# Attention's loop in a gated encoder step: lows, transposes and values at other steps, one reciprocal for two heads, shared score tiles, LayerNorm's own temporaries

## The chip, the cores and the metric

The kernel runs on one core of one Trainium2 chip. Its time is the device time of one execution in microseconds (us); lower is better. Of several executions the median is given. One further execution is recorded by the profiler; it has its own time.

## The reference

One step of an encoder layer with two branches on one RMS-normed input `h` (1024 prompt tokens, 32 sample tokens with 512 cached keys, model width 1024, 16 heads of 64):

```python
q = rmsnorm(h @ w_q, q_g) / 8 ; k = rmsnorm(h @ w_k, k_g) ; v = h @ w_v       # per head
logf = log_sigmoid(h @ w_f + b_f) ; c = cumsum(logf)
s = q @ k.T + c[t] - c[s]            # causal mask
o = softmax(s) @ v
u = (h @ w_ua) * sigmoid(h @ w_ub)
conv = causal_dwconv(u, w_dw, width 31) + b_dw
ya = (o * silu(h @ w_ga)) @ w_pa
yb = (silu(layernorm(conv, ln_g, ln_b)) * silu(h @ w_gb)) @ w_pb
y = x + (sigmoid(h @ w_ma) * ya + sigmoid(h @ w_mb) * yb) @ w_out
```

Everything is float32 outside; inside, each product is made of three matmuls of high and low halves (hi x hi, lo x hi, hi x lo).

## The kernel before

Activations lie with channels on the 128 partitions and the 1056 tokens along the free dimension, in three chunks of 352 columns (`CH`). The kernel runs in stages: input split and the projections u, v, k, q and the first gates (0 to 581 us); **attention, interleaved with the rest of the gate projections** (581 to 1021 us); output projections (from 1021 us). The change lies in the second stage alone.

*Units.* A unit is one block of 128 queries of one head: `units` runs over the 8 pairs of heads, within a pair over the blocks in the order `MORD = (3, 1, 2, 0)` (two query blocks each, so i = 6, 7, 2, 3, 4, 5, 0, 1), and within a block over the two heads (e = 0, 1). A unit has w = 128 (i + 1) keys. That gives 128 units, 16 for a pair of heads; here "narrow" means i up to 3, w up to 512. At loop step k these stand, in this order:

- `scores` of unit k (L1220 to L1222): matmuls into a PSUM tile psS, 1024 fp32 columns wide, of which there are two;
- `high` of unit k-2 (L1243, ScalarE): the probabilities times a factor, as f16, into the tile PH (four buffers);
- half of the step's fill: pieces of gate projections (L188), three matmuls each, whose number goes with the width of the unit;
- `top` of k (L1226, VectorE, the row maximum) and `soft` of k (L1231, ScalarE, the exponential into P, four buffers, with the row sum);
- `low` of k-2: the rest after the high part, on VectorE for the first head (L1252), on GpSimd in two instructions for the second (L1249, L1250);
- `factor` of k-1 (L1236, L1237, VectorE): one reciprocal of the row sum and one scaling;
- the step's events: loads of the next heads, and for each block of four units `values` (L1280, matmuls with the transposed probabilities PT) at `LAG` = 6 steps after the first unit's step + 3, and `gated` a step later;
- the other half of the fill, then `turn` of k-2 (L1260): a transposing DMA from PH to PT, issued by SyncE.

Each engine takes its instructions in the order in which they are written here; SyncE's queue, too, which also issues the weight loads, the next heads' loads and the stores of gate tiles.

*Beats.* Each piece of fill is a beat. A beat runs what is due: the preparation of the next weights (`stage`: squares and their sum; `total`: a small matmul; `power`; `split` and `rest`: L141, L146), and taps. A tap (L379, VectorE) is one of 31 terms of the depthwise convolution for one channel block f; `pace["rate"]` (`R_A` = 0.15 in this stage) says how many run in a beat. After the last tap of f the result y is stored (`kept`), and `sums(f)` subtracts the shift from y in place (L345) and adds y to the running mean (L352) and, later, its square (L359). After channel block 7 these give LayerNorm's statistics: `layernorm` runs one piece in each loop step and takes its temporaries from the tiles `t` (`t352`, three buffers), which also hold the gate projections' results until they are stored.

Of the kernel before, what the change touches and what calls it, by code (L numbers as in the profile page):

```python
# [34 lines left out]
R_U, R_V, R_QK, R_G, R_A = 0.21, 0.18, 0.165, 0.23, 0.15  # L35
NWARM = 34
PS14 = 2.0 ** 14
LAG = 6
# [19 lines left out]
def build(tc, xT, xt, wv, wf, ckT, cv, clT, stT, vec, cst, yT, kT, vO, lfO, cpT, csT):  # L58
# [33 lines left out]
    class Batch:  # L92
# [21 lines left out]
        def stage(self, i):  # L114
# [6 lines left out]
            if i == 1:  # L121
                nc.gpsimd.tensor_copy(self.topb, self.tops)
# [103 lines left out]
    def begin():  # L226
# [10 lines left out]
        elif b.n == 2:  # L237
# [5 lines left out]
            if lag > 1:  # L243
                jobs[:2] = [(23, b.total), (23, b.power)]
# [124 lines left out]
    def conv_taps(f):  # L369
        u = us.pop(f)  # L370

        def tap(i):
# [9 lines left out]
            if i == KC - 1:  # L382
                kept(f, y)

# [3 lines left out]
        if f == 7:  # L388
            taps.extend(pend + items)
# [788 lines left out]
    taps.extend(sums(7))  # L1178
# [26 lines left out]
    class Unit:  # L1205
# [6 lines left out]
        def scores(self):  # L1212
# [3 lines left out]
            self.ps = ps = psS.tile([128, T], F32, name="psS", tag="S")  # L1216
# [7 lines left out]
        def top(self):  # L1224
            self.nm = ap.tile([128, 3], F32, name="nm", tag="nm", bufs=6)
            nc.vector.tensor_reduce(self.nm[:, 0:1], self.ps[:, :self.w], axis=AX.X, op=ALU.max, negate=True)  # L1226

        def soft(self):
            self.P = ap.tile([128, T], F32, name="P", tag="P", bufs=4)
            with tc.issue_after(sides["tables"].ins):  # L1230
                nc.scalar.activation(self.P[:, :self.w], self.ps[:, :self.w], AF.Exp, bias=self.nm[:, 0:1],  # L1231
                                     accum_out=self.nm[:, 1:2])

        def factor(self):
            nm = self.nm
            nc.vector.reciprocal(nm[:, 2:3], nm[:, 1:2])  # L1236
            nc.vector.tensor_scalar(nm[:, 2:3], nm[:, 2:3], PS14, None, op0=ALU.mult)  # L1237

        def high(self):
            n = self.i + 1  # L1240
            self.H = ap.tile([128, 8, 2, 128], F16, name="PH", tag="PH", bufs=4)
            self.P3 = self.P[:, :self.w].rearrange("p (j k) -> p j k", j=n)
            nc.scalar.mul(self.H[:, :n, 0, :], self.P3, self.nm[:, 2:3])  # L1243

        def low(self):
            n = self.i + 1
            f = self.nm[:, 2:3]
# [50 lines left out]
    def layernorm():  # L1298

        shift = sides["shift"]  # L1300
# [4 lines left out]
        for c in range(3):  # L1305
            sl = csl(c)
            t = t352("t", 3)
# [3 lines left out]
            nc.tensor.matmul(pm[:, :CH], ones_f, rstd[:, sl], start=True, stop=True)  # L1311
            nc.vector.scalar_tensor_tensor(rstd[:, sl], pm[:, :CH], 1.0 / D, t, op0=ALU.mult, op1=ALU.subtract)
            nc.vector.tensor_add(mean[:, sl], mean[:, sl], shift[:, sl])
            nc.vector.tensor_scalar(rstd[:, sl], rstd[:, sl], EPS, None, op0=ALU.add)
        for c in range(6):
            sl = slice(c * CH // 2, c * CH // 2 + CH // 2)
            v, y = rstd[:, sl], t352("t", 3)[:, :CH // 2]
# [3 lines left out]
            w = t352("t", 3)[:, :CH // 2]  # L1321
# [19 lines left out]
    rate = (24 * NFILL - 30) / sum(u.w + WB for u in units)  # L1341
# [453 lines left out]
```

## Time and profile before

| | |
|---|---|
| median of three executions | 1311.63 us (1310.82 to 1311.67) |
| profiled execution | 1317.82 us, span of its instructions 1314.7 us |
| TensorE (PE) busy | 1249.7 us, 95% |
| VectorE (DVE) busy | 1013.1 us, 77% |
| ScalarE (ACT) busy | 732.9 us, 56% |
| GpSimd (POOL) busy | 632.4 us, 48% |
| DMA | 213.66 MB, mean 163 GB/s |

The rows of the trace in this document are read so. A group of instructions: line of the kernel, engine, operation, tiles (out<-in), shapes, count | busy us, mean ns of one | the engine's idle time just before them, and what ended it. A wait: who waited <- for whom: us in total, times, longest. A stretch of busy time: start:end, length, then for PE, PEld (weight loads), DVE, ACT and POOL busy us (count), the granted TensorE clock, the DMA engines' busy share, GB/s. A line of the timeline: start us, length us, engine, line, operation, tiles, count, and in brackets the idle time before it.

### The profile page before, as it was taken

The page shows a single profiled execution, that of the slowest core. Times are in us where ns is not written, and L with a number is a line of the kernel's source. Part 1 is how long each engine was busy: PE and PEld are TensorE (multiplying, and loading weights), DVE is VectorE, ACT ScalarE, POOL GpSimd, SP SyncE. Part 2 cuts the span into 40 slices and gives each one's busy share as a digit, 9 for nine tenths or more (in the row PEclk, how much of TensorE's full clock was granted, in tenths as well). Part 3 has the DMA queues.
Part 4 walks back from the last instruction along what each step waited for, and adds up shares of the span by engine and source line. Part 5 has one row for each costly group of instructions (what it writes and reads, how often), then busy time and mean ns, then how long its engine had stood idle before and what let it go on. Part 6 is the DMA issues. An engine that isn't in the chain of part 4 may idle for free.

```text
span 1314.7 us, 25051 instructions
## 1 busy us (share of the span) xinstructions
PE 1249.7 (95%) x9270; PEld 929.2 (71%) x9270; DVE 1013.1 (77%) x1526; ACT 732.9 (56%) x1353; POOL 632.4 (48%) x590
## 2 busy tenths in 40 slices
PE   8999999999999999998888898979799999999998
PEld 5677776666666666665555565646466799999998
DVE  6799899888988998889778798857566496156664
ACT  6555555867686865556556555656565665133320
POOL 4057574728474741015545355443444277165562
PEclk9999999999999999999989999989899999999999
DMA  7344242425343464629988898978987987444462
GB/s 258 100 131 118 79 129 62 122 66 142 95 118 109 116 196 156 195 82 192 201 200 188 197 227 203 211 181 191 205 189 158 345 263 242 146 132 156 119 213 70
DMA packets 275161, 213.66 MB, mean 163 GB/s; under 512 B 188512, under 2 KB 241632, under 8 KB 275040
## 3 DMA queue, kind: packets, MB, share of 16 engines
q1 hardware_dynamic: 274896, 212.01, 60.9%
q8 instruction: 72, 1.18, 0.4%
q14 instruction: 49, 0.40, 0.1%
q10 hardware_dynamic: 144, 0.07, 0.0%
HBM read 115.04 MB, written 59.22 MB: 133 GB/s over the span
## 4 chain that ended last, share of the span: by engine, by line
PE 71%; DVE 8%; issue 6%; DMA 6%; POOL 5%; ACT 3%; SPq 0%; POOLq 0%; ACTq 0%; DVEq 0%
PE pj L188 52%; PE pjv L813 7%; PE pj L1625 6%; DMA PT<-PH 4%; PE po L1280 2%; POOL PH L1250 2%; POOL P L1249 2%; DVE PH L1252 2%; DVE nm L1226 1%; DVE wl L146 1%; DVE y L379 1%; DMA s_y<-y 1%; POOL wh L141 1%; PE psS L1220 1%; PE psS L1221 1%
## 5 line engine op out<-in xcount | busy, mean ns | idle before, releaser
L188 PE MATMUL pj<-xh,wh 128*128 128x352 f16 (+2 forms) x1536 | 485.0, 316 | 0.6 <-DVE qn L959 0.5
L188 PE MATMUL pj<-xl,wh 128*128 128x352 f16 (+2 forms) x1536 | 484.0, 315 | 1.4 <-DVE xl L599 1.3
L188 PE MATMUL pj<-xh,wl 128*128 128x352 f16 (+2 forms) x1536 | 484.3, 315 | 0.1
L188 PEld LDWEIGHTS <-wh 128*128 128x128 f16 x3072 | 302.5, 98 | 166.1 <-issue 3.6
L379 DVE SCALAR_TENSOR_TENSOR y<-u,vec_t,y 128x1086 f32<-128x1086 f32 x240 | 360.2, 1502 | 3.9 <-ACT y L376 0.9
L188 PEld LDWEIGHTS <-wl 128*128 128x128 f16 x1536 | 151.3, 98 | 69.1 <-issue 1.0
L146 DVE SCALAR_TENSOR_TENSOR wl<-raw,sc,wh 128x384 f16<-128x384 f32 x188 | 142.7, 780 | 26.7 <-ACT wh L143 25.3
L1231 ACT ACTIVATE P<-psS,nm 128x1024 f32<-128x1024 f32 (+7 forms) x128 | 94.0, 734 | 111.7 <-DVE nm L1236 53.9
L1249 POOL TENSOR_SCALAR P<-P,nm 128x896 f32<-128x896 f32 (+3 forms) x64 | 65.8, 1028 | 181.7 <-ACT PH L1243 177.2
L1243 ACT ACTIVATE PH<-P,nm 128x1024 f16<-128x1024 f32 (+7 forms) x128 | 98.5, 770 | 46.7 <-DMA PT<-PH 24.5
L1226 DVE TENSOR_REDUCE nm<-psS 128x1 f32<-128x1024 f32 (+7 forms) x128 | 96.1, 751 | 30.7 <-PE psS L1222 30.5
L180 POOL TENSOR_TENSOR wl<-raw,wh 128x384 fp32r<-128x384 f32 (+1 forms) x51 | 64.4, 1287 | 72.8 <-ACT wh L177 50.9
L1220 PE MATMUL psS<-KB,QB 128*128 128x512 f16 (+2 forms) x192 | 63.7, 332 | 35.7 <-ACT P L1231 35.4
L1250 POOL TENSOR_TENSOR PH<-P,PH 128x896 f16<-128x896 f32 (+3 forms) x64 | 89.5, 1398 | 4.9
L944 POOL TENSOR_TENSOR sql<-sqf,sqh 128x352 fp32r<-128x352 f32 x48 | 54.0, 1127 | 66.0 <-ACT sqh L941 65.8
L1252 DVE SCALAR_TENSOR_TENSOR PH<-P,nm,PH 128x896 f16<-128x896 f32 (+3 forms) x64 | 61.2, 956 | 28.6 <-ACT PH L1243 28.6
L1280 PE MATMUL po<-PT,Vh 128*64 128x256 f16 (+1 forms) x640 | 63.6, 285 | 15.0 <-DMA PT<-PH 15.0
L813 PE MATMUL pjv<-vwh,xh 128*128 128x260 f16 x256 | 70.1, 274 | 0.0
L813 PE MATMUL pjv<-vwl,xh 128*128 128x260 f16 x256 | 70.0, 273 | 0.0
L813 PE MATMUL pjv<-vwh,xl 128*128 128x260 f16 x256 | 69.9, 273 | 0.0
L970 POOL TENSOR_TENSOR ql<-qn,qh 128x352 f16<-128x352 f32 (+1 forms) x48 | 63.8, 1344 | 8.8 <-ACT qh L969 8.6
L119 ACT ACTIVATE junk<-raw 128x1024 bf16<-128x1024 f32 x62 | 65.0, 1049 | 0.1
(299 smaller groups left out, 2628.7 us busy)
## 6 DMA issues: line engine op xcount, KB each, us to landing
raw<-wf SPq DMA_DIRECT2D x92, 512.0 KB
kT<-kun SPq DMA_DIRECT2D x8, 528.0 KB
s_ga<-t SPq DMA_DIRECT2D x24, 176.0 KB
s_gb<-t SPq DMA_DIRECT2D x24, 176.0 KB
s_ma<-t SPq DMA_DIRECT2D x24, 176.0 KB
s_mb<-t SPq DMA_DIRECT2D x24, 176.0 KB
sma<-s_ma SPq DMA_DIRECT2D x24, 176.0 KB
y<-s_y SPq DMA_DIRECT2D x8, 528.0 KB
```

The source lines that it names most:

```text
L146: nc.vector.scalar_tensor_tensor(wl[:, ks, :], raw[:, ks, :], self.s[:, i:i + 1], wh[:, ks, :], op0=ALU.mult, op1=ALU.subtract)
L188: nc.tensor.matmul(ps, a[:, kt, :], b(kt, sl), start=(first and n == 0), stop=(last and n == N - 1))
L379: t = nc.vector.scalar_tensor_tensor(y, u[:, i:i + CW], w, y, op0=ALU.mult, op1=ALU.add)
L813: nc.tensor.matmul(ps[:, :VC], a, b, start=(n == 0), stop=(n == 23))
L1226: nc.vector.tensor_reduce(self.nm[:, 0:1], self.ps[:, :self.w], axis=AX.X, op=ALU.max, negate=True)
L1231: nc.scalar.activation(self.P[:, :self.w], self.ps[:, :self.w], AF.Exp, bias=self.nm[:, 0:1], accum_out=self.nm[:, 1:2])
L1243: nc.scalar.mul(self.H[:, :n, 0, :], self.P3, self.nm[:, 2:3])
L1249: nc.gpsimd.tensor_scalar(self.P3, self.P3, f, 1.0, op0=ALU.mult, op1=ALU.mult)
L1250: nc.gpsimd.tensor_sub(self.H[:, :n, 1, :], self.P3, self.H[:, :n, 0, :])
L1252: nc.vector.scalar_tensor_tensor(self.H[:, :n, 1, :], self.P3, f, self.H[:, :n, 0, :], op0=ALU.mult, op1=ALU.subtract)
L1280: nc.tensor.matmul(po[64 * e:64 * e + 64, 128 * ii.start:256], v[:, j, 64 * e:64 * e + 64], pt[:, ii, e, j, x, :], start=(j == 0 and n == ...
L1625: nc.tensor.matmul(pss[c][:, :HC], a[:, k, :], x, start=(not more and kt == 0 and n == 0), stop=(kt == 3 and n == 2), skip_group_check=more)
```

## The change

- `soft`, `top`: the small tile `nm` is one for both heads of a pair (maxima in columns 0 and 1, sums in 2 and 3, factors in 4 and 5). `factor` runs once for two heads, at the even steps.
- `scores`: for narrow units both heads of a pair share one psS tile, the first head in columns 0 to 511, the second in 512 to 1023.
- `high` is of unit k-3 instead of k-2, PH has five buffers (`PHB`); `low` is of k-3 and stands at the step's end; `turn` is called for two units at a time, k-5 and k-4, at even steps; the values come two steps later (`LAG` = 8); the loop has four more steps.
- The gate fill in the loop: 36 pieces instead of 30 are left for its end.
- Taps: rate 0.18 instead of 0.15; for f = 7 the sums of block 6 come after eight taps instead of three; the sums of block 7 come 28 beats after its last tap instead of at once.
- Weights in this stage: the sum of squares is cast on ScalarE instead of GpSimd, and its `total` comes at beat 19 instead of 23.
- `layernorm` has temporaries of its own (`lt`, three buffers of 176 columns), and its second sum is made in six pieces instead of three.

```diff
-R_U, R_V, R_QK, R_G, R_A = 0.21, 0.18, 0.165, 0.23, 0.15
+R_U, R_V, R_QK, R_G, R_A = 0.21, 0.18, 0.165, 0.23, 0.18
-LAG = 6
+LAG = 8
+PHB = 5
...
-                nc.gpsimd.tensor_copy(self.topb, self.tops)
+                if sides.get("cast") == "pool":
+                    nc.scalar.copy(self.topb, self.tops)
+                else:
+                    nc.gpsimd.tensor_copy(self.topb, self.tops)
...
-                jobs[:2] = [(23, b.total), (23, b.power)]
+                jobs[:2] = [(19, b.total), (23, b.power)]
...
             if i == KC - 1:
                 kept(f, y)
+                if f == 7:
+                    later(28, lambda: [fn() for fn in sums(7)])
...
         if f == 7:
-            taps.extend(pend + items)
+            taps.extend(items[:8] + pend + items[8:])
...
-    taps.extend(sums(7))
...
-            self.ps = ps = psS.tile([128, T], F32, name="psS", tag="S")
+            if i > 3:
+                self.ps = ps = psS.tile([128, T], F32, name="psS", tag="S")
+            else:
+                if not self.e:
+                    self.pair.ps = psS.tile([128, T], F32, name="psS", tag="S")
+                self.ps = ps = self.pair.ps[:, 512 * self.e:512 * self.e + 512]
...
         def top(self):
-            self.nm = ap.tile([128, 3], F32, name="nm", tag="nm", bufs=6)
-            nc.vector.tensor_reduce(self.nm[:, 0:1], self.ps[:, :self.w], axis=AX.X, op=ALU.max, negate=True)
+            e = self.e
+            if not e:
+                self.pair.nm = ap.tile([128, 6], F32, name="nm", tag="nm", bufs=4)
+            self.nm = self.pair.nm
+            nc.vector.tensor_reduce(self.nm[:, e:e + 1], self.ps[:, :self.w], axis=AX.X, op=ALU.max, negate=True)
...
-            nc.vector.reciprocal(nm[:, 2:3], nm[:, 1:2])
-            nc.vector.tensor_scalar(nm[:, 2:3], nm[:, 2:3], PS14, None, op0=ALU.mult)
+            nc.vector.reciprocal(nm[:, 4:6], nm[:, 2:4])
+            nc.vector.tensor_scalar(nm[:, 4:6], nm[:, 4:6], PS14, None, op0=ALU.mult)
...
-            self.H = ap.tile([128, 8, 2, 128], F16, name="PH", tag="PH", bufs=4)
+            self.H = ap.tile([128, 8, 2, 128], F16, name="PH", tag="PH", bufs=PHB)
...
-        for c in range(3):
-            sl = csl(c)
-            t = t352("t", 3)
+        for c in range(6):
+            sl = slice(c * CH // 2, c * CH // 2 + CH // 2)
+            t = part()
...
-            v, y = rstd[:, sl], t352("t", 3)[:, :CH // 2]
+            v, y = rstd[:, sl], part()
...
-            w = t352("t", 3)[:, :CH // 2]
+            w = part()
...
-    rate = (24 * NFILL - 30) / sum(u.w + WB for u in units)
+    rate = (24 * NFILL - 36) / sum(u.w + WB for u in units)
...
-    for k in range(len(units) + 2):
-        u, v, w = [unit(k - n) for n in range(3)]
+    for k in range(len(units) + 6):
+        u, x = unit(k), unit(k - 3)
         if u:
             u.scores()
-        if w:
-            w.high()
+        if x:
+            x.high()
         fill_for(rate * (u.w + WB) / 2 if u else 2.0)
         if u:
             u.top()
             u.soft()
-        if w:
-            w.low()
-        if v:
-            v.factor()
+        if k % 2 == 0:
+            if unit(k - 1):
+                unit(k - 1).factor()
+            for y in (unit(k - 5), unit(k - 4)):
+                if y:
+                    y.turn()
         for fn in events.pop(k, ()):
             fn()
         fill_for(rate * (u.w + WB) / 2 if u else 2.0)
         aged(1)
-        if w:
-            w.turn()
+        if x:
+            x.low()
```

(`part()` makes a tile `lt` of 128 x 176.) Three places show how this moves instructions. The first is VectorE's order at units 51 to 53 (a second head of 1024 keys, then a narrow pair), where nm<-psS is the maximum, PH<-P,nm,PH the low part and nm<-nm the factor. Before:

```order
L1226 TENSOR_REDUCE nm<-psS 128x1
L1236 RECIPROCAL nm<-nm 128x1
L1237 TENSOR_SCALAR nm<-nm 128x1
L379 SCALAR_TENSOR_TENSOR y<-u,vec_t,y 128x1086
L1226 TENSOR_REDUCE nm<-psS 128x1
L1252 SCALAR_TENSOR_TENSOR PH<-P,nm,PH 128x8x128
L1236 RECIPROCAL nm<-nm 128x1
L1237 TENSOR_SCALAR nm<-nm 128x1
L1226 TENSOR_REDUCE nm<-psS 128x1
L1236 RECIPROCAL nm<-nm 128x1
L1237 TENSOR_SCALAR nm<-nm 128x1
```

and now:

```order
L1239 TENSOR_REDUCE nm<-psS 128x1
L1267 SCALAR_TENSOR_TENSOR PH<-P,nm,PH 128x7x128
L383 SCALAR_TENSOR_TENSOR y<-u,vec_t,y 128x1086
L1239 TENSOR_REDUCE nm<-psS 128x1
L1250 RECIPROCAL nm<-nm 128x2
L1251 TENSOR_SCALAR nm<-nm 128x2
L1303 SCALAR_TENSOR_TENSOR ot<-po,vsc,ga 128x256
L1239 TENSOR_REDUCE nm<-psS 128x1
L383 SCALAR_TENSOR_TENSOR y<-u,vec_t,y 128x1086
L1267 SCALAR_TENSOR_TENSOR PH<-P,nm,PH 128x8x128
L1239 TENSOR_REDUCE nm<-psS 128x1
L1250 RECIPROCAL nm<-nm 128x2
```

The low part stood behind the maximum of an even unit and now stands ahead of the next even unit's maximum, a unit's age older; the factor's two instructions come once for two maxima and are two columns wide.

The second is TensorE's order at the first head of the second narrow block (unit 6 of the first pair of heads), with the semaphores that an instruction waits for. Before:

```order
L1220 LDWEIGHTS QB_7032
L1220 MATMUL psS<-KB_7034,QB_7032 128x512 [waits Activation_49]
L1221 LDWEIGHTS QA_7031
L1221 MATMUL psS<-KA_7033,QA_7031 128x512
L1222 LDWEIGHTS identm
L1222 MATMUL psS<-mask_178,identm 128x128
```

and now:

```order
L1230 LDWEIGHTS QB_7032
L1230 MATMUL psS<-KB_7034,QB_7032 128x512 [waits PE_49]
L1231 LDWEIGHTS QA_7031
L1231 MATMUL psS<-KA_7033,QA_7031 128x512
L1232 LDWEIGHTS identm
L1232 MATMUL psS<-mask_178,identm 128x128
```

This matmul waited for ScalarE (the exponential of unit 4) and now waits for nothing new on ScalarE. The matmuls of the second heads of narrow pairs wait for a ScalarE count in both; before it is the count set by the exponential two units back, now by the exponential one unit back, that of the first head in the same tile.

The third is VectorE's order around the end of the taps of channel block 7 (y<-u,vec_t,y is a tap, y<-y,shift the subtraction in place, wl<-raw,sc,wh a low half of weights). Before:

```order
L379 SCALAR_TENSOR_TENSOR y<-u,vec_t,y 128x1086
L146 SCALAR_TENSOR_TENSOR wl<-raw,sc,wh 128x384
L1226 TENSOR_REDUCE nm<-psS 128x1
L1236 RECIPROCAL nm<-nm 128x1
L1237 TENSOR_SCALAR nm<-nm 128x1
L146 SCALAR_TENSOR_TENSOR wl<-raw,sc,wh 128x384
L345 TENSOR_TENSOR y<-y,shift 128x1024
L345 TENSOR_TENSOR y<-y,shift 128x32
L146 SCALAR_TENSOR_TENSOR wl<-raw,sc,wh 128x256
```

and now, at unit 73, with the last tap at unit 66:

```order
L1239 TENSOR_REDUCE nm<-psS 128x1
L1250 RECIPROCAL nm<-nm 128x2
L1251 TENSOR_SCALAR nm<-nm 128x2
L1303 SCALAR_TENSOR_TENSOR ot<-po,vsc,ga 128x256
L150 SCALAR_TENSOR_TENSOR wl<-raw,sc,wh 128x256
L1239 TENSOR_REDUCE nm<-psS 128x1
L1267 SCALAR_TENSOR_TENSOR PH<-P,nm,PH 128x4x128
L349 TENSOR_TENSOR y<-y,shift 128x1024
L349 TENSOR_TENSOR y<-y,shift 128x32
L356 TENSOR_TENSOR mean<-mean,y 128x1024
L356 TENSOR_TENSOR mean<-mean,y 128x32
```

The subtraction followed the last tap after one unit's instructions; now seven units lie between them, and the sum into the mean follows it at once.

More of the change, by code (lines that the diff above doesn't have):

```diff
@@ L1224, in top @@
         def top(self):
-            self.nm = ap.tile([128, 3], F32, name="nm", tag="nm", bufs=6)
-            nc.vector.tensor_reduce(self.nm[:, 0:1], self.ps[:, :self.w], axis=AX.X, op=ALU.max, negate=True)
+            e = self.e
[3 more added lines that the diff above has]
+            nc.vector.tensor_reduce(self.nm[:, e:e + 1], self.ps[:, :self.w], axis=AX.X, op=ALU.max, negate=True)
         def soft(self):
+            e = self.e
             self.P = ap.tile([128, T], F32, name="P", tag="P", bufs=4)
             with tc.issue_after(sides["tables"].ins):
-                nc.scalar.activation(self.P[:, :self.w], self.ps[:, :self.w], AF.Exp, bias=self.nm[:, 0:1],
-                                     accum_out=self.nm[:, 1:2])
+                nc.scalar.activation(self.P[:, :self.w], self.ps[:, :self.w], AF.Exp, bias=self.nm[:, e:e + 1],
+                                     accum_out=self.nm[:, 2 + e:3 + e])
         def factor(self):
             nm = self.nm
-            nc.vector.reciprocal(nm[:, 2:3], nm[:, 1:2])
-            nc.vector.tensor_scalar(nm[:, 2:3], nm[:, 2:3], PS14, None, op0=ALU.mult)
+            nc.vector.reciprocal(nm[:, 4:6], nm[:, 2:4])
+            nc.vector.tensor_scalar(nm[:, 4:6], nm[:, 4:6], PS14, None, op0=ALU.mult)
         def high(self):
             n = self.i + 1
-            self.H = ap.tile([128, 8, 2, 128], F16, name="PH", tag="PH", bufs=4)
+            self.H = ap.tile([128, 8, 2, 128], F16, name="PH", tag="PH", bufs=PHB)
             self.P3 = self.P[:, :self.w].rearrange("p (j k) -> p j k", j=n)
-            nc.scalar.mul(self.H[:, :n, 0, :], self.P3, self.nm[:, 2:3])
+            self.f = self.nm[:, 4 + self.e:5 + self.e]
+            nc.scalar.mul(self.H[:, :n, 0, :], self.P3, self.f)
         def low(self):
             n = self.i + 1
-            f = self.nm[:, 2:3]
+            f = self.f
             if self.e:
@@ L1298, in layernorm, with part @@
     def layernorm():
+        def part():
+            return ap.tile([128, CH // 2], F32, name="lt", tag="lt", bufs=3)
         shift = sides["shift"]
@@ L1310, in layernorm @@
             pm = psT.tile([128, 512], F32, name="psn", tag="T")
-            nc.tensor.matmul(pm[:, :CH], ones_f, rstd[:, sl], start=True, stop=True)
-            nc.vector.scalar_tensor_tensor(rstd[:, sl], pm[:, :CH], 1.0 / D, t, op0=ALU.mult, op1=ALU.subtract)
+            nc.tensor.matmul(pm[:, :CH // 2], ones_f, rstd[:, sl], start=True, stop=True)
+            nc.vector.scalar_tensor_tensor(rstd[:, sl], pm[:, :CH // 2], 1.0 / D, t, op0=ALU.mult, op1=ALU.subtract)
             nc.vector.tensor_add(mean[:, sl], mean[:, sl], shift[:, sl])
```

## The prediction

> **What bounds the kernel now.** I read the page's head and slices first, then the busy time by stretch, then who waited for whom in the stretch that the change touches.
>
> ```profile
> span 1314.7 us, 25051 instructions
> PEclk9999999999999999999989999989899999999999
> 581.00:1012.00 431.00, 379.48 (x2978) 247.72 (x2977) 328.72 (x650) 254.15 (x514) 196.70 (x174) 0.95 0.89 193
> 1021.00:1230.00 209.00, 209.00 (x1335) 200.49 (x1336) 117.84 (x135) 91.69 (x121) 106.52 (x78) 1.00 0.62 204
> PE psS L1220 <- ACT P L1231: 35.4, 25, 4.8
> PE po L1280 <- DMA PT<-PH: 15.0, 12, 2.5
> ```
>
> The first two rows are the page's; then come two rows of busy time by stretch (start:end, length, then PE, weight loads, DVE, ACT, POOL, the granted clock, the DMA share); then two of the waits (total, times, longest). The attention loop runs from 581 to 1012 us. There TensorE works 379.5 of 431 us, and the clock granted to it is 0.95; after the loop it works all of the time at 1.00. So TensorE bounds the kernel, and what the loop can give back is its idle time, 51.5 us, and its clock, 5% of 431. Nearly all of the idle time ends in two ways: a score matmul waits for the exponential that must empty its PSUM tile (35.4), or the values' matmuls wait for a transposed tile (15.0). One of the 128 loop steps takes 431/128 = 3.37 us.
>
> **Part A, the long waits that go.** The DVE queue is in order, and two things block it.
>
> ```profile
> DVE y L345 <- DMA s_y<-y: 10.9, 2, 5.7
> DVE t L1322 <- DMA s_mb<-t: 11.9, 3, 5.2
> 675.15 0.22 PE L1220 MATMUL psS<-KB,QB 128*128 128x128 f16 x1 [1.68 <-ACT P L1231]
> 678.23 0.27 PE L1220 MATMUL psS<-KB,QB 128*128 128x128 f16 x1 [1.85 <-ACT P L1231]
> 861.34 0.48 PE L1220 MATMUL psS<-KB,QB 128*128 128x384 f16 x1 [2.90 <-ACT P L1231]
> 867.23 0.32 PE L1220 MATMUL psS<-KB,QB 128*128 128x384 f16 x1 [2.48 <-ACT P L1231]
> 921.16 0.32 PE L1220 MATMUL psS<-KB,QB 128*128 128x384 f16 x1 [2.19 <-ACT P L1231]
> 932.18 0.38 PE L1220 MATMUL psS<-KB,QB 128*128 128x512 f16 x1 [2.24 <-ACT P L1231]
> 950.35 0.26 PE L1220 MATMUL psS<-KB,QB 128*128 128x128 f16 x1 [2.72 <-ACT P L1231]
> 953.26 0.27 PE L1220 MATMUL psS<-KB,QB 128*128 128x128 f16 x1 [0.68 <-ACT P L1231]
> ```
>
> First, the subtraction of the shift overwrites `y` right after its store was issued, and DVE stands for 5.7 and 5.2 us until the store has read it. The row maxima behind it are late, so the exponentials are, and TensorE waits right after: 1.68 + 1.85 + 2.90 + 2.48 = 8.91 us. The change puts eight taps rather than three between store and subtraction for channel block 6, and 28 beats for block 7. Second, LayerNorm shares its temporaries with the gates' tiles, which a store must empty. After those waits TensorE stands 2.19 + 2.24 + 2.72 + 0.68 = 7.83 us. Temporaries of their own have no store behind them. What is late next in both places is the ordinary chain of maximum and exponential; I take both sums as gone, 16.74 us.
>
> These waits cost more than their length, because the clock drops behind them:
>
> ```profile
> 676.80:683.50 6.70, 5.27 (x38) 3.50 (x38) 3.99 (x11) 4.68 (x12) 3.10 (x3) 0.50 1.01 217
> 861.10:864.40 3.30, 3.06 (x12) 1.54 (x12) 3.27 (x8) 1.67 (x4) 1.75 (x1) 0.50 0.69 127
> 868.00:871.30 3.30, 3.30 (x21) 1.74 (x20) 2.22 (x6) 2.64 (x6) 0.17 (x1) 0.50 0.92 210
> 922.60:925.90 3.30, 3.30 (x20) 1.89 (x21) 2.12 (x6) 3.27 (x9) 1.07 (x3) 0.50 0.68 125
> 932.80:936.10 3.30, 3.30 (x15) 1.75 (x13) 0.81 (x3) 2.28 (x5) 3.22 (x5) 0.50 1.15 279
> 949.90:956.60 6.70, 5.57 (x37) 3.45 (x38) 6.46 (x16) 4.41 (x11) 2.38 (x2) 0.50 0.74 172
> ```
>
> Each stretch lies at or just behind one of the waits above and has a granted clock of 0.50. TensorE is busy 23.80 us in the six; at full clock that work takes half, so 11.9 us go with the waits. **A = -28.6 us** (bounds: 0, if other waits take their place, and -28.6).
>
> The Trainium skill ("TensorE: Matmul & The Clock Gate", section "HAM oscillation — how this bites in real kernels") gives as its abstract rule "no PE-idle gaps >~3.4µs". By it none of these gaps would have cost clock, and A would be -16.7 us. The trace does not agree: behind the gap of 2.24 us the clock is 0.50, so the rows decide.
>
> **Part B, values later.** The values of a block of four scores move from two to four loop steps behind their last high part, and the transposes move too: the second head's from the end of step +2 to the middle of step +5, the values from +6 to +8.
>
> ```profile
> 605.17 5.52 DMA PT<-PH
> 714.16 4.36 DMA PT<-PH
> ACT PH L1243 <- DMA PT<-PH: 24.5, 17, 5.0
> ```
>
> The first two rows are from the chain of waits: 4.4 to 5.5 us from a transpose's issue to its landing. Three steps are 10.1 us, and the low part, which ended just ahead of the transpose before, now has a step and more to finish. Against it, SP's queue is in order, and the transposes now stand behind two more steps of gate stores, weight loads and next heads' loads; the narrow steps are much shorter than the mean. The tile PH has five buffers for four, and its reuse lies five units back, so ACT's wait of 24.5 us has about the cover it had. Bounds: -15.0 (every wait goes) and +15.0 (twice as many). I take two thirds of the waits: **B = -10 us**.
>
> **Part C, the shared score tile: a wait that is added.** For blocks up to 512 keys both heads of a pair now write one PSUM tile. In the built program, the second head's first score matmul then waits for the ACT count that the *first head's exponential of the same pair* sets; before, for that of the unit two back. That holds in all 32 narrow pairs. In return the first head of the next narrow pair waits for no new exponential. What the new wait would cost on the old timeline is the end of the first head's exponential less the start of the second head's matmul; the first of the 32 pairs and the last:
>
> ```profile
> 596.42 0.33 PE L1220 MATMUL psS<-KB,QB 128*128 128x384 f16 x1
> 597.71 0.58 ACT L1231 ACTIVATE P<-psS,nm 128x384 f32<-128x384 f32 x1 [1.92 <-DVE nm L1226]
> 1005.85 0.27 PE L1220 MATMUL psS<-KB,QB 128*128 128x256 f16 x1
> 1006.42 0.46 ACT L1231 ACTIVATE P<-psS,nm 128x256 f32<-128x256 f32 x1
> ```
>
> 597.71 + 0.58 - 596.42 = 1.87 us, and 1.03 us at the end. Over all 32 it is 47.7 us, 1.49 on average: today TensorE runs ahead of DVE and ACT at each of these places. Behind the waiting matmul stand the gate projections that fill TensorE, so nothing covers it. But the two waits of a block of four share one lag: once TensorE has let DVE and ACT catch up at the first, little is left at the second. I take one wait in two: **C = +16 x 1.49 = +23.8 us** (bounds 0 and +47.7).
>
> The Trainium skill ("PSUM — Partial Sum Buffer", section "Summary: rules for kernel authors") says for reading PSUM during matmuls to target a different bank. The halves of the shared tile are 512 fp32 columns each, so by that rule the second head need not wait and C would be 0; no run here shows a shared tile, and the wait stands in the program.
>
> **Part D, the smaller ones.**
>
> ```profile
> L1236 DVE RECIPROCAL nm<-nm 128x1 f32<-128x1 f32 x128 | 19.6, 153 | 0.0
> L1237 DVE TENSOR_SCALAR nm<-nm 128x1 f32<-128x1 f32 x128 | 19.7, 154 | 4.4
> L379 DVE SCALAR_TENSOR_TENSOR y<-u,vec_t,y 128x1086 f32<-128x1086 f32 x47 | 74.6, 1586 | 0.0
> DVE PH L1252 <- ACT PH L1243: 28.6, 30, 3.3
> DVE sc L162 <- PE tot L128: 8.9, 6, 3.0
> ```
>
> One reciprocal and one scaling for two heads: 64 x (153 + 154) = 19.6 us of DVE work less. The low parts stand a step's half later, so most of DVE's 28.6 us of waiting for ACT's high part goes; the total of the squares four beats earlier takes most of the 8.9. None of this is TensorE's own time. It can shorten what is left of the score waits, 35.4 - 16.7 = 18.7 us. Against it, the 47 taps (74.6 us) come 20% denser and end around unit 66 instead of 80, and a low part now stands right ahead of an even unit's maximum. Bounds 0 and -18.7; nearer to the first: **D = -5 us**.
>
> Costs at nothing: the probabilities' four buffers are now freed by POOL one step before reuse instead of two:
>
> ```profile
> L1243 ACT ACTIVATE PH<-P,nm 128x1024 f16<-128x1024 f32 (+7 forms) x128 | 98.5, 770 | 46.7 <-DMA PT<-PH 24.5 <-ACT P L1231 6.3 <-issue 6.3
> L1249 POOL TENSOR_SCALAR P<-P,nm 128x896 f32<-128x896 f32 (+3 forms) x64 | 65.8, 1028 | 181.7 <-ACT PH L1243 177.2 <-DMA s_mb<-t 4.4
> L1250 POOL TENSOR_TENSOR PH<-P,PH 128x896 f16<-128x896 f32 (+3 forms) x64 | 89.5, 1398 | 4.9
> L122 POOL CAST topb<-tops 128x2 bf16<-128x2 f32 x11 | 2.8, 258 | 36.4 <-ACT junk L119 36.4
> ```
>
> 0.77 + 1.03 + 1.40 = 3.20 us against a step of 3.37: covered on average; uncovered by a microsecond for each of the 32 wide odd units it would be a delay of ACT, which the two score tiles still hide. The cast of the squares goes from POOL to ACT, 11 x some 0.2 us; LayerNorm's second sum in six pieces for three streams the same columns. The loop leaves 36 gate pieces instead of 30 for the tail, where they cover the last transposes. All before 575 us and after 1021 us is unchanged.
>
> **Sum.** -28.6 - 10 + 23.8 - 5 = -19.8 us. The profiled execution took 1317.8 us (span 1314.7 and 3.1 around it), so it becomes 1298.0; it stands 6.2 above the median of 1311.6, and the same step from the median gives **1292 us**.
>
> **The rivals.**
> 1. *Slower: the shared tile takes over.* Each of the 32 waits costs its full 1.49 us, plus the low part (0.956, below) that now stands ahead of the maximum it waits for, less the spared 0.31: 32 x 2.14 = 68.5. -43.6 + 68.5 = +24.9, 1337 us. It is slower than before from 1.36 us a wait on. For it: today's lag is at least that in the mean. Against it: the lag is shared, and DVE has less to do. The middle of this case is 1325.
>
> ```profile
> L1252 DVE SCALAR_TENSOR_TENSOR PH<-P,nm,PH 128x896 f16<-128x896 f32 (+3 forms) x64 | 61.2, 956 | 28.6 <-ACT PH L1243 28.6
> ```
>
> 2. *The transposes gain nothing*, since they wait in SP's queue as long as the values were moved: B = 0, 1302 us. For it: narrow steps.
> 3. *DVE is no longer late*: without the blocked stretches and the 19.6 us, the maximum follows the scores at once and C is near 4: 1272 us.
> 4. *The clock does not come back*: waits at the narrow pairs halve it as those of A did, so that 11.9 stays: 1304 us. By the rule of the Trainium skill quoted above no wait of a microsecond or two could; here gaps of 2 us do, so it is small but there.
>
> **How the numbers follow.** Forecast 0.38, rivals 0.17, 0.17, 0.20, 0.08. The range leaves out most of rival 1 above 1318 and the end of rival 3 below 1268. A measurement of this kernel tells about 0.2% (2.6 us) from no change. Rivals 2 and 4 lie partly within or above it: faster 0.77, same 0.06, slower 0.17.
>
> **What would show it.** Right: no wait of DVE on the store of `y` or on gate tiles; granted clock in the loop above 0.97; score waits that sit on the second head of narrow pairs, some 24 us; waits for transposes around 5. Wrong: those second-head waits at 44 us or more; the values' waits unchanged; a new wait of the exponential for POOL that reaches TensorE.

## The result: 1300.1 us, 0.9909 of the time before

The changed kernel takes 1300.1 us (median of four executions, 1296.9 to 1301.2), the kernel before in the same comparison 1311.65 (1310.8 to 1312.1). The ratio is 0.9909, with a 95% interval of 0.989 to 0.9927: a gain of 12 us, against a forecast of 1292 and a range of 1268 to 1318. The profiled execution took 1299.3 us; its span went from 1314.7 to 1297.2 us.

The page's head and the busy time by stretch of the changed kernel, in the columns of before:

```profile
span 1297.2 us, 25077 instructions
PEclk9999999999999999999999999999999999999999
581.00:1012.00 431.00, 388.12 (x3119) 254.48 (x3118) 330.23 (x539) 260.68 (x534) 184.25 (x171) 0.97 0.91 202
1021.00:1218.00 197.00, 197.00 (x1256) 194.33 (x1255) 114.52 (x127) 86.59 (x119) 102.20 (x75) 1.00 0.59 192
```

No slice of the clock stands below 9 any more; three did. TensorE's idle time in the stretch from 581 to 1012 us went from 51.5 to 431 - 388.1 = 42.9 us. After the loop it works all of the time, as before. The second quantity is the clock. The mean granted clock over the whole span says what it costs at most: (1 - clock) x span, called the clock loss from here on. The row of all cores, for before and then for the changed kernel:

```profile
core 0: 1314.7 us, clock 0.982
```

```profile
core 0: 1297.2 us, clock 0.988
```

That is 0.018 x 1314.7 = 23.7 us before and 0.012 x 1297.2 = 15.6 us after. Idle time -8.6 and clock -8.1 make -16.7 of the -17.5 us by which the span fell between these two executions.

The medians differ by less, and the clock accounts for most of that. The profiled execution of before has a clock as low as any on record: its 32 executions beside the experiments below lie between 0.982 and 0.988, with 18.3 us of clock loss in the mean. The four executions of the change lie between 0.986 and 0.988, with 17.2 us. So over all executions the clock gave back about 1 us, less than these means can tell, and nearly all of the gain of 12 us lies outside it.

Who waited for whom, from 575 to 1022 us of the changed kernel:

```profile
PE psS L1230 <- ACT P L1245: 41.6, 25, 3.2
PE po L1295 <- DMA PT<-PH: 0.5, 2, 0.3
DVE nm L1239 <- PE psS L1232: 66.1, 51, 3.4
DVE PH L1267 <- ACT PH L1258: 4.8, 5, 1.8
ACT P L1245 <- POOL PH L1265: 20.0, 13, 3.4
ACT P L1245 <- DVE PH L1267: 17.2, 8, 3.7
ACT PH L1258 <- DMA PT<-PH: 5.1, 4, 1.8
```

The values no longer wait for transposes (15.0 to 0.5), the high parts hardly (24.5 to 5.1), VectorE's low parts neither (28.6 to 4.8), and the waits on the store of `y` and on gate tiles are gone from the list. The score waits went the other way, from 35.4 to 41.6, and exponentials now wait 37.2 us for low parts (3.7 before, 2.8 and 0.9 for GpSimd's two instructions).

Counted by the unit that waits, 40.6 of the 41.6 us stand at second heads of narrow blocks, the place that the forecast named. They are spread otherwise than it assumed: a narrow block of four units has two pairs, and 6.7 us stand at its first pair, 33.9 us at its second. Before, score waits stood at wide and narrow units and at both heads. One such place in order of time; units 38 and 39 are the two heads of one narrow pair:

```profile
704.04 2.79 POOL L1265 TENSOR_TENSOR PH<-P,PH 128x896 f16<-128x896 f32 x1
704.93 0.22 PE L1232 MATMUL psS<-mask,identm 128*128 128x128 f16 x1
705.01 2.90 DVE L1267 SCALAR_TENSOR_TENSOR PH<-P,nm,PH 128x1024 f16<-128x1024 f32 x1
707.84 0.68 DVE L1239 TENSOR_REDUCE nm<-psS 128x1 f32<-128x512 f32 x1
708.91 0.68 ACT L1245 ACTIVATE P<-psS,nm 128x512 f32<-128x512 f32 x1
709.74 0.38 PE L1230 MATMUL psS<-KB,QB 128*128 128x512 f16 x1 [3.24 <-ACT P L1245]
```

The first head's scores end at 705.15 with the mask. VectorE starts the low part of a wide unit, four units back, just ahead of the maximum, and that takes 2.90 us beside GpSimd's subtraction; so the maximum comes at 707.84, the exponential ends at 709.59, and the second head's scores, which need the shared tile, have stood for 3.24 us.

### The profile page after: what moved, and what is told of

Same layout as the page of the kernel before. It is cut to its first block, busy times and chain, and to the rows that moved or that the text cites. A ratio compares the mean times of both kernels' runs of the same rounds, so it can differ in the third digit from the quotient of the medians.

```text
span 1297.2 us, 25077 instructions
## 1 busy us (share of the span) xinstructions
PE 1240.8 (96%) x9276; PEld 924.2 (71%) x9276; DVE 1009.1 (78%) x1407; ACT 735.1 (57%) x1367; POOL 609.1 (47%) x579
## 4 chain that ended last, share of the span: by engine, by line
PE 79%; DVE 10%; DMA 4%; issue 3%; ACT 3%; POOL 1%; SPq 0%; DVEq 0%; ACTq 0%; POOLq 0%
PE pj L192 56%; PE pjv L819 7%; PE pj L1645 6%; PE po L1295 3%; DVE nm L1239 2%; DVE y L383 2%; PE psS L1230 2%; DMA PT<-PH 2%; DVE PH L1267 2%; PE psS L1231 2%; DVE wl L150 1%; ACT P L1245 1%; ACT PH L1258 1%; DMA pf<-s_cs 1%; PE pst L930 1%
## 5 line engine op out<-in xcount | busy, mean ns | idle before, releaser
L383 DVE SCALAR_TENSOR_TENSOR y<-u,vec_t,y 128x1086 f32<-128x1086 f32 x240 | 356.0, 1484 | 4.1 <-ACT y L380 1.1
L150 DVE SCALAR_TENSOR_TENSOR wl<-raw,sc,wh 128x384 f16<-128x384 f32 x188 | 131.3, 720 | 25.2 <-ACT wh L147 25.1
L1239 DVE TENSOR_REDUCE nm<-psS 128x1 f32<-128x1024 f32 (+7 forms) x128 | 96.2, 752 | 67.9 <-PE psS L1232 66.1
L1264 POOL TENSOR_SCALAR P<-P,nm 128x896 f32<-128x896 f32 (+3 forms) x64 | 55.4, 866 | 189.6 <-ACT PH L1258 157.5
L1230 PE MATMUL psS<-KB,QB 128*128 128x512 f16 (+2 forms) x192 | 63.4, 330 | 42.3 <-ACT P L1245 41.6
L184 POOL TENSOR_TENSOR wl<-raw,wh 128x384 fp32r<-128x384 f32 (+1 forms) x51 | 62.9, 1260 | 76.2 <-ACT wh L181 51.5
L1265 POOL TENSOR_TENSOR PH<-P,PH 128x896 f16<-128x896 f32 (+3 forms) x64 | 86.7, 1355 | 5.1
L1267 DVE SCALAR_TENSOR_TENSOR PH<-P,nm,PH 128x896 f16<-128x896 f32 (+3 forms) x64 | 66.1, 1032 | 6.1 <-ACT PH L1258 4.8
L141 POOL TENSOR_SCALAR sc<-sc,back 128x2 f32<-128x2 f32 (+1 forms) x37 | 21.3, 577 | 94.6 <-DVE sc L166 90.5
L1038 ACT ACTIVATE t<-pj,sc 128x352 f32<-128x352 f32 x72 | 39.5, 549 | 46.2 <-PE pj L192 43.0
```

The lines of the kernel that those rows point to most:

```text
L150: nc.vector.scalar_tensor_tensor(wl[:, ks, :], raw[:, ks, :], self.s[:, i:i + 1], wh[:, ks, :], op0=ALU.mult, op1=ALU.subtract)
L383: t = nc.vector.scalar_tensor_tensor(y, u[:, i:i + CW], w, y, op0=ALU.mult, op1=ALU.add)
L1230: nc.tensor.matmul(ps[:, ksl], QB[:, qsl], KB[:, ksl], start=True, stop=False)
L1239: nc.vector.tensor_reduce(self.nm[:, e:e + 1], self.ps[:, :self.w], axis=AX.X, op=ALU.max, negate=True)
L1265: nc.gpsimd.tensor_sub(self.H[:, :n, 1, :], self.P3, self.H[:, :n, 0, :])
L1267: nc.vector.scalar_tensor_tensor(self.H[:, :n, 1, :], self.P3, f, self.H[:, :n, 0, :], op0=ALU.mult, op1=ALU.subtract)
```

## The experiments

Three theories were to be told apart. **Theory 1**: the shared tile's wait keeps the remaining idle time. **Theory 2**: VectorE and ScalarE are late because of where the low part stands, and the wait would only move. **Theory 3**: the four buffers of the probabilities, held longer by the later low parts, make ScalarE late. Each group of runs was timed together with the kernel before on one chip, so times are compared by their ratio to it.

| kernel | median us | ratio (95%) | PE idle 581 to 1012 | clock loss | clock loss, mean of all executions | score waits |
|---|---|---|---|---|---|---|
| the change | 1300.1 | 0.9909 (0.989 to 0.9927) | 42.9 | 15.6 | 17.2 | 41.6 |
| e1 own score tiles | 1285.2 | 0.9788 (0.9765 to 0.981) | 33.2 | 10.3 | 12.3 | 24.5 |
| e2 both heads' scores together | 1285.6 | 0.9792 (0.9769 to 0.9814) | 31.8 | 15.4 | 14.6 | 19.7 |
| e3 before + A | 1296.6 | 0.987 (0.9848 to 0.9893) | 41.3 | 14.3 | 11.0 | 23.9 |
| e4 low part half a step earlier | 1300.8 | 0.9907 (0.9883 to 0.9931) | 44.7 | 15.6 | 17.8 | 43.6 |
| e5 five P, four PH | 1303.0 | 0.992 (0.9899 to 0.9941) | 49.1 | 13.0 | 16.1 | 48.4 |
| e6 = e1 + e5 | 1286.2 | 0.9785 (0.9763 to 0.9807) | 33.6 | 11.6 | 10.6 | 26.5 |
| e7 = e2 + e5 | 1284.6 | 0.9778 (0.9757 to 0.98) | 28.8 | 15.4 | 13.8 | 13.4 |
| e8 before + A + values later | 1290.4 | 0.981 (0.9786 to 0.9834) | 41.7 | 7.7 | 9.5 | 41.3 |
| e9 = e2 + five P, five PH | 1290.3 | 0.9832 (0.9812 to 0.9853) | 31.2 | 15.5 | 15.5 | 12.0 |
| e10 = e1 + five P, five PH | 1288.2 | 0.9818 (0.9801 to 0.9835) | 31.4 | 12.9 | 11.6 | 20.3 |
| e11 the change + five P, five PH | 1300.8 | 0.9912 (0.9893 to 0.993) | 40.6 | 15.6 | 17.1 | 39.9 |
| e12 before + A + shared tile | 1306.0 | 0.9944 (0.9927 to 0.9961) | 48.1 | 14.3 | 17.2 | 45.0 |

The idle time, the clock loss and the score waits are those of the profiled execution; before has 51.5, 23.7 and 35.4 us. The mean clock loss is worked out from the clock and span of each execution; single executions of one kernel differ by up to 13 us in it (e11, 0.981 to 0.991), so means closer than some 3 us are not told apart.

### e1: a score tile for each unit

```diff
-            if i > 3:
-                self.ps = ps = psS.tile([128, T], F32, name="psS", tag="S")
-            else:
-                if not self.e:
-                    self.pair.ps = psS.tile([128, T], F32, name="psS", tag="S")
-                self.ps = ps = self.pair.ps[:, 512 * self.e:512 * self.e + 512]
+            self.ps = ps = psS.tile([128, T], F32, name="psS", tag="S")
```

> The change with its shared score tile undone alone: every unit of 128 queries and one head takes a score tile of its own, as before the change. Theory 1 (the second head's wait for the first head's exponential of the same pair keeps the remaining idle time): the score waits, 41.6 us after the change, fall to 12 or less in total, half-clock stretches go from 8 to 3 or fewer, and the time goes from 1300 to between 1260 and 1280. Theory 2 (DVE and ACT are simply late, because the low part stands ahead of the even unit's maximum and runs beside POOL's): the waits move to other units of the block and stay above 30 us; 1292 to 1302.

The time fell to 1285.2: the shared tile costs 0.9909 - 0.9788 = 1.2%, 16 us. Neither theory met its numbers. The waits of e1:

```profile
PE psS L1225 <- ACT P L1240: 24.5, 20, 3.7
PE po L1290 <- DMA PT<-PH: 8.5, 5, 4.3
ACT P L1240 <- DVE PH L1262: 30.8, 14, 3.8
ACT P L1240 <- POOL PH L1260: 22.5, 14, 4.4
```

Of 41.6 us of score waits 17.1 went, and 8.0 came back at once as waits of the values for transposes. In the two profiled executions that leaves 9.7 us of idle time and 5.3 us of clock loss as the price of the tile. The second heads of narrow blocks have gone from 40.6 us to 16.6, all of it at the second pairs, although these heads now wait for the exponential two units back alone. So the wait that the change's trace shows at the tile is two to three times what the removal of the tile brings.

### e2: the scores of both heads together

```diff
-        if u:
+        if u and not (u.e and u.i < 4):
             u.scores()
+            if u.i < 4:
+                unit(k + 1).scores()
```

> The change with the shared score tile kept, but the scores of both heads of a narrow block issued together, ahead of the first head's exponential, so that nothing waits for the exponential of its own pair; the first head of a narrow pair then waits for the exponential two or three units back. Theory 1: score waits of 15 us or less, 1260 to 1282. Theory 2: the waits move to the first heads and stay above 30; 1292 to 1302. Against both: the first head's maximum now waits for the second head's scores too, at most 0.8 us in each of 32 pairs, and the fillers that stood between are behind it.

1285.6 us, the same as e1, with the tile still shared; the score waits and the time again lie between the two theories' numbers. So it is not the sharing that costs, but the order: the second head's scores written behind the first head's exponential, on which the program then makes them wait. The score waits that remain are of another kind:

```profile
PE psS L1230 <- ACT P L1245: 19.7, 10, 3.9
PE po L1295 <- DMA PT<-PH: 11.9, 7, 3.5
```

15.0 of the 19.7 us stand at the second head of the wide pair right behind the first narrow block of a pair of heads; none is left at a narrow second head.

### e3: the kernel before with part A alone

```diff
+                if f == 7:
+                    later(28, lambda: [fn() for fn in sums(7)])
...
-            taps.extend(pend + items)
+            taps.extend(items[:8] + pend + items[8:])
...
-    taps.extend(sums(7))
...
+        def part():
+            return ap.tile([128, CH // 2], F32, name="lt", tag="lt", bufs=3)
```

LayerNorm's second sum runs in six pieces, as in the change.

> The kernel before with part A of the change alone: the second LayerNorm sum of channel block 6 behind eight taps, that of block 7 behind 28 beats, and LayerNorm's temporaries of its own in six pieces. The prediction's step A says -28.6 us (16.7 of idle time and 11.9 of clock): 1283. If other waits take the clock back, as after the whole change: -17, 1295. If the maxima are late anyway: 1308 to 1312.

1296.6 us, 1.3% or 17 us less than before. Both waits of VectorE are gone from the list of waits.

```profile
581.00:1012.00 431.00, 389.72 (x3135) 257.57 (x3133) 345.95 (x673) 259.38 (x524) 205.70 (x182) 0.97 0.94 203
core 0: 1295.7 us, clock 0.989
```

TensorE's idle time fell by 10.2 us and the clock loss by 23.7 - 14.3 = 9.4 (by 8.2 in the means of all executions of the group, 19.2 to 11.0): A is right in kind, and some 60% of its size. The score waits fell by 11.5, not by 16.7. At the eight places of the forecast they did go: 0.85 of 16.7 us is left there. But two waits grew elsewhere by 5.0 us together, and both stand behind work that A moved:

```profile
863.34 2.33 DVE L352 TENSOR_TENSOR mean<-mean,y 128x1024 f32<-128x1024 f32 x2
865.59 0.68 DVE L1227 TENSOR_REDUCE nm<-psS 128x1 f32<-128x512 f32 x1
867.19 0.38 PE L1221 MATMUL psS<-KB,QB 128*128 128x512 f16 x1 [2.87 <-ACT P L1232]
719.22 3.89 POOL L359 TENSOR_TENSOR rstd<-rstd,y 128x1024 f32<-128x1024 f32 x2
720.31 2.70 DVE L146 SCALAR_TENSOR_TENSOR wl<-raw,sc,wh 128x384 f16<-128x384 f32 x1
725.01 0.22 PE L1221 MATMUL psS<-KB,QB 128*128 128x128 f16 x1 [3.25 <-ACT P L1232]
```

In the first three rows the sums of block 7 (3.65 us with the subtraction at 862.09) stand right ahead of a row maximum; no score wait stood there before. In the others GpSimd's sum of squares of block 6, which ran at 690 us before, has come beside a low half of weights ahead of a maximum; that takes 2.70 us now, and the wait behind it is 3.25 us in place of 1.16. The same low half before:

```profile
727.28 0.61 DVE L146 SCALAR_TENSOR_TENSOR wl<-raw,sc,wh 128x384 f16<-128x384 f32 x1
```

### e4: the low part half a step earlier

```diff
             u.soft()
+        if x:
+            x.low()
         if k % 2 == 0:
...
         aged(1)
-        if x:
-            x.low()
```

> The change with the low part issued half a step earlier, right behind the unit's own exponential, as it stood in the step before; nothing else is moved. Theory 2 (a low part of up to 2.9 us right ahead of the even unit's maximum makes the first head's exponential late): the score waits fall from 41.6 to 25 or less, and the time by 10 us or more. Theory 1: the waits are set by the order of scores, maximum and exponential in the pair itself, and stay above 35; within 4 us of the change.

1300.8 us and 43.6 us of score waits: nothing changed. The numbers are theory 1's, but theory 2 does not fall with them. The low part of a first head still stands between the same two maxima, now ahead of the taps and not behind them. Between the scores and the maximum of the 16 second narrow pairs lie 30.0 us in the change, of which VectorE spends 19.9 in low parts and 5.9 in taps; in e4 it is 31.8, with 14.7 in low parts and 10.7 in taps. So half a step did not bring the low part out of the maximum's way.

### e5, e6 and e7: five buffers for the probabilities, four for the high parts

```diff
-PHB = 5
+PHB = 4
...
-            self.P = ap.tile([128, T], F32, name="P", tag="P", bufs=4)
+            self.P = ap.tile([128, T], F32, name="P", tag="P", bufs=5)
```

> The change with five buffers for the probabilities instead of four, and four instead of five for the high and low parts (the memory allows no more). An exponential then waits for the low part of five units back, issued two steps earlier, not one; a high part waits for the transpose of four units back. Theory 3 (the exponential's waits for POOL's and DVE's low parts, 37.2 us on ACT after the change, feed the score waits): those fall below 12 us, the score waits from 41.6 to 30 or less, and the time from 1300 to 1292 or less. Theory 1 (the shared tile alone decides): score waits stay above 36, within 4 us of 1300. If the four high-part buffers are too few, ACT's waits for transposes rise above 20 us and hide the answer.

> A score tile for each unit as in e1 (1285.2), and five buffers for the probabilities as in e5. Theory 3: with the shared tile gone the low parts' hold on the buffers is what is left (ACT waits 53.3 us for it in e1), so score waits fall from 24.5 to 12 or less and the time to 1278 or less. Theory 1: those waits are slack of ACT; 1283 to 1288.

> Scores of both heads together as in e2 (1285.6), and five buffers for the probabilities as in e5. Theory 3: score waits from 19.7 to 10 or less, 1278 or less. Theory 1: 1283 to 1288.

None gained that can be measured against its base (e5 against the change, e6 against e1, e7 against e2). In e5 the exponentials' waits for low parts vanish, and this takes their place:

```profile
ACT PH L1258 <- DMA PT<-PH: 35.1, 22, 4.3
```

37.2 us of ScalarE's waits are exchanged for 30 others (5.1 to 35.1): four buffers for the high parts are too few, and that hides the answer. e9 to e11 were made to get it.

### e8: before with A and the later values

```diff
-LAG = 6
+LAG = 8
+PHB = 5
...
             v.factor()
+        if k % 2 == 0:
+            for y in (unit(k - 5), unit(k - 4)):
+                if y:
+                    y.turn()
...
-        if w:
-            w.turn()
```

> The kernel before with part A (1296.6 in e3) and part B: the values eight steps behind, transposes in even steps for both heads, five buffers for the high and low parts; the high and low parts, the factor of each head and the score tiles stay as before. The prediction's B of -10: 1287, with the values' waits, 22.3 us in e3 on TensorE's two queues, at 7 or less. If the values' waits only move to other waits of the same units: 1294 to 1299. Against e1, which has one factor for both heads and the later low parts besides: if those are worth D's -5, e8 is at 1290; if they cost (probabilities held for longer), e8 is below 1283.

The cut leaves out A's edit, which is that of e3, and the loop's longer end. 1290.4 us: 0.981 against e3's 0.987, 0.6% or 8 us, between the forecast's 1287 and the 1294 to 1299 of waits that only move. The values' waits for transposes are gone, but the idle time is not:

```profile
PE psS L1222 <- ACT P L1233: 41.3, 33, 4.2
581.00:1012.00 431.00, 389.31 (x3174) 256.19 (x3172) 344.29 (x680) 265.64 (x531) 205.93 (x182) 0.99 0.95 210
core 0: 1288.9 us, clock 0.994
```

Idle time is 41.7 us as in e3; what the values no longer waited for, the scores did. They wait more often and for less (33 times, 1.25 us in the mean). Between the profiled executions the gain is in the clock, 7.7 us of clock loss in place of 14.3. The other executions do not bear that out: e3's profiled one has the lowest clock of its four (0.989; the others have 0.992 and 0.993, with spans of 1294.1 to 1294.9), and e8's four others have 0.991 to 0.993 with spans of 1283.3 to 1288.8, so at nearly the same clock e8 is shorter by 5 us or more. In the means the clock loss falls by 1.5 us only. What else fell no profile shows. Between e8 and e1, which has one reciprocal for both heads, the later low parts, the denser taps and the other weight steps besides, lie 0.981 - 0.9788 = 0.2%, 3 us, within both intervals.

### e9, e10 and e11: five buffers of both kinds

```diff
-            self.P = ap.tile([128, T], F32, name="P", tag="P", bufs=4)
+            self.P = ap.tile([128, T], F32, name="P", tag="P", bufs=5)
...
-            t = t352("t", 3)
+            t = t352("t", 2)
...
-            self.gate = ap.tile([128, 256], F32, name="ga", tag="ga", bufs=2)
+            self.gate = ap.tile([128, 256], F32, name="ga", tag="ga", bufs=1)
...
-            ot = ap.tile([128, 256], F32, name="ot", tag="ot", bufs=2)
+            ot = ap.tile([128, 256], F32, name="ot", tag="ot", bufs=1)
```

> Scores of both heads together as in e2, five buffers for the probabilities and five for the high and low parts; the memory comes from one buffer less for the gates' tiles t, for the loaded gate and for the gated output. Unlike e7, ACT's waits for the low part are not exchanged for waits for transposes. Theory 3 (the late low parts hold ACT, and ACT holds TensorE): both kinds of ACT's waits together at 40 us or less (52 in e2, 64 in e7), TensorE's idle time in the loop from 31.6 to 22 or less, 1270 to 1279. If the buffers only pass one lateness on: 1281 to 1288, as e2 and e7.

> The same memory as in e9 with a score tile for each unit. Theory 3: TensorE's idle time in the loop from 33.0 (e1) to 23 or less, 1272 to 1280. Otherwise as e1 and e6, 1283 to 1288.

> The change with its shared score tile and the memory of e9. Theory 1 (with the shared tile, it alone sets the score waits): they stay above 36 us and the time within 4 us of 1300. Theory 3: 30 or less, 1293 or less.

e11 is the clean test of theory 3. Exponentials wait for no low part any more, and high parts for next to no transpose; they wait for VectorE instead, and TensorE as before:

```profile
ACT P L1245 <- DVE nm L1250: 63.9, 42, 4.4
ACT P L1245 <- DVE nm L1239: 41.1, 41, 3.1
ACT PH L1258 <- DMA PT<-PH: 0.4, 1, 0.4
PE psS L1230 <- ACT P L1245: 39.9, 25, 3.6
```

1300.8 us against 1300.1: theory 3 falls for the change. e9 and e10 gained nothing either (e9 is slower than e2 by 0.4%); in both, ScalarE waits 12 and 20 us more for the stores of the gates' tiles that gave up a buffer, so for them the answer is less clean.

### e12: the shared tile on the step of before

The edit is that of e1 the other way round, on the kernel of e3.

> The kernel before with part A and the shared score tile alone; the step, its low parts, transposes and values as before. It prices part C on another step than e1 did. The prediction's C of +23.8: 1296.6 (e3) becomes 1320. As between e1 and the change (+15): 1312. If the shared tile costs only where the low part stands late: 1294 to 1300.

1306.0 us: 0.9944 against e3's 0.987, +0.7% or 10 us. So the tile costs on either step.

```profile
581.00:1012.00 431.00, 382.95 (x3089) 251.46 (x3088) 343.76 (x665) 258.02 (x520) 199.42 (x179) 0.97 0.90 198
PE psS L1226 <- ACT P L1237: 45.0, 26, 4.9
```

Here 31.1 of the 45.0 us stand at the first narrow pair and 11.6 at the second, the reverse of the change: this is the sharing of a lag that the forecast assumed.

## Why the prediction was right, term by term

The forecast of a gain held, with the time 8 us too low. Two terms were off, in opposite directions: A brought 12 us less than forecast, and C cost 8 us less. That the sum came so near is in part luck, since these errors cancel. By its number alone the result, 1300, lies nearer to rivals 2 (1302) and 4 (1304) than to 1292; only the terms tell them apart. Taken from the ratios, times 1312 us:

| term | predicted | measured | from |
|---|---|---|---|
| A, the long waits | -28.6 | -17 | e3 against before |
| B, values later | -10 | -8 | e8 against e3 |
| D, the smaller ones | -5 | -3 | e1 against e8 |
| C, the shared tile | +23.8 | +16 (+10 on the step of before) | the change against e1 (e12 against e3) |
| sum | -19.8 | -12 | the change against before |

Each difference of two ratios is uncertain by some 0.3%, 4 us, so B and D are not told from their forecasts, and D not from nothing. A and C are.

**A is the term that was mis-sized most.** The step "I take both sums as gone" was right for the eight places, where 15.9 of 16.7 us went (e3's profile). What it left out is that the moved sums need a place: they stand ahead of other maxima now, and two waits there grew by 5.0 us. In all 10.2 of 16.7 us of idle time went, and some 8 to 9 of 11.9 us of clock. This is A's price on the step of before. In the changed kernel the moved sums run at 688 to 703 and 820 to 833 us, and the only score wait there is one of 0.6 us; what A is worth on that step no run shows.

**C's mechanism was right, its size was not.** The waits sit where the program's dependency said, at second heads of narrow pairs, and e1, e2 and e12 show that this dependency is the cause of the 16 and the 10 us. "One wait in two" was not the shape: on the new step the first pair of a block waits little, since its maximum follows the scores by a mean of 0.25 and 0.37 us (the two narrow blocks), and the second pair's by 1.7 and 2.05, because low parts of wide units and taps stand ahead of it on VectorE (25.8 of the 30.0 us counted under e4). In waits the term is 40.6 us, not far from the 44 at which the forecast called itself wrong. Of these, 16.6 stand in e1, too, and what goes there comes back for more than half: 8.0 as waits of the values, 6.9 as score waits of other units. So the tile costs 9.7 us of idle time (42.9 against 33.2), not 23.8. It also costs some 5 us of clock, which the forecast had put at nothing in this term, although its own A priced gaps of this length with their clock: clock loss is 17.2 us in the mean against e1's 12.3, and in e12 17.2 against e3's 11.0.

**B** came in size, but its way is not shown: in e8 the values no longer wait, yet the idle time is that of e3, and the clock accounts for a small part (see e8). The high parts' wait for transposes, which the forecast took as about unchanged, fell from 24.5 to 5.1 us in the change, but not in e8 (33.0), where the high parts stand as before. In the whole change the values' waits fell to 0.5 us; in e1, without the shared tile, they are 8.5 again, so a part of that was the shared tile's doing: TensorE, held at the scores, came to the values later.

**What was costed at nothing** was nothing, though not for want of waits: exponentials wait 37.2 us for low parts, 20.0 of them for GpSimd, and e11, which removes these waits, takes the same time. The cast on ScalarE, LayerNorm's pieces and the longer tail were not run apart.

**The rivals.** The shared tile did not take over (rival 1): its price stayed under the gains. The transposes did gain (rival 2). VectorE is still late (rival 3), in the wide units' low parts and the taps. Rival 4, that the clock does not come back, is for the most part what happened: in the profile eight half-clock stretches are left in the loop, each at one of the new waits of 2.2 to 3.3 us, and over all executions the clock loss went from 18.3 to 17.2 us, where 11.9 us were forecast to go. A alone brought 8 us of it (e3), and the tile took 5 to 6 back.

**Expected signs.** Clock above 0.97 in the loop: just missed, since the eight stretches of 3.41 us make 1 - 13.6/431 = 0.968, shown as 0.97. Waits for transposes around 5: 0.5. Second-head waits of some 24: 40.6.

**A version that beats both kernels** is the change with e1's edit or e2's: 0.979 of the time before, against 0.991. Five buffers for the probabilities add nothing measurable.

**Open.** 33 us of idle time remain in e1. That VectorE's taps and low parts ahead of the maximum make them is argued from the timeline, not shown: no run took work from VectorE, or put the maximum ahead of the taps and the low part, so theory 2 is open for what is left. Why the tile's price is 16 us on one step and 10 on the other was not followed up; the intervals (12 to 20 and 6 to 13 us) touch.

## What to carry to other kernels

When two users share a tile, write all their writes ahead of the first read; in e2 that alone gave back what the sharing cost. A wait's length in a trace is not its price: here 40.6 us of waits at the tile cost 16 us, of which some 5 were clock, and 16.7 us of waits behind a blocked queue were worth 17 us, half of it clock. Ask what the waiting engine would meet next, where moved work will stand, and price by removing one dependency at a time. In this loop a removed wait often returned as another (values' waits as score waits in e8, buffer waits as transposes' in e5, waits behind the sums at their new places in e3). And one profiled execution is one draw of the clock: compare the clock over all executions before it is made a cause.

## What the runs showed of the hardware

**Half clock after two microseconds.** Three of the changed kernel's half-clock stretches, each at the end of a score wait or just behind it (2.24, 3.24 and 2.35 us):

```profile
628.70:632.10 3.40, 3.40 (x30) 2.33 (x28) 2.20 (x3) 1.92 (x7) 1.29 (x1) 0.50 1.22 224
710.60:714.00 3.40, 3.40 (x22) 1.78 (x21) 3.07 (x3) 1.94 (x6) 1.39 (x1) 0.51 1.09 235
785.70:789.10 3.40, 3.07 (x22) 1.99 (x23) 2.27 (x2) 2.46 (x8) 2.43 (x2) 0.50 1.09 251
```

Counted over the loops of all fourteen traces: of 101 waits of TensorE of 2.0 us or more, 80 had a half-clock stretch begin within them or up to 3.5 us behind them; of 268 shorter ones (0.15 us and up), 15. In the 3.4 us ahead of each of the 86 stretches TensorE had been idle for at least 1.77 us, in one gap or several. The rule quoted in the prediction from the Trainium skill ("TensorE: Matmul & The Clock Gate", section "HAM oscillation — how this bites in real kernels"), that asks for no gap above about 3.4 us, is too lax here: half of that in idle time was enough.

**VectorE beside GpSimd.** The low part of 1024 columns, before and after:

```profile
L1252 DVE SCALAR_TENSOR_TENSOR PH<-P,nm,PH 128x1024 f16<-128x1024 f32 x8 | 11.3, 1410 | 5.3 <-ACT PH L1243 5.3
```

```profile
L1267 DVE SCALAR_TENSOR_TENSOR PH<-P,nm,PH 128x1024 f16<-128x1024 f32 x8 | 14.6, 1828 | 0.7 <-DMA ga<-s_ga 0.5 <-ACT PH L1258 0.2
```

In the changed kernel three of the eight, with GpSimd idle, took 1.27 us each; three that ran for more than half of their time beside GpSimd's instructions took 2.5 us in the mean. They do not meet more often than before: of all 64 low parts on VectorE 25 run beside GpSimd for some time in either kernel, and together they take 61.2 us before and 66.1 now. The Trainium skill ("SBUF — State Buffer", section "Who interferes with whom") says that a VectorE instruction with two inputs from SBUF contends with a GpSimd instruction that reads SBUF; the trace agrees for the three, with 2.5 against 1.27 us. It does not always show on VectorE: one of the eight of before ran for 0.92 of its time beside a GpSimd subtraction and took 1.29 us, while that subtraction took 2.93 us.
